# Explicit order at both ends of the SwiGLU groups of a decoder block in float32

## The chip, the cores and the metric

One core of a Trainium2 chip. The metric is the device time of one execution in microseconds (us). The engines are TensorE (PE; its weight loads are listed as PEld), VectorE (DVE), ScalarE (ACT), GpSimd (POOL) and SyncE (SP), whose queue issues nearly all loads from HBM. Each engine runs its own instructions in order; semaphores tie the engines together.

## The reference, cut to what matters

A decoder block: a mixer (pooling heads beside differential attention), then a gated feed-forward part, each with a norm before and after it. Sequence 256, width D = 2048, inner width DFF = 5632, everything in float32. The change is in the feed-forward part alone:

```python
hn = rms_norm(h, pre_ffn_norm[l])
ff = (jax.nn.silu(hn @ w_gate[l]) * (hn @ w_up[l])) @ w_down[l]
h = h + rms_norm(ff, post_ffn_norm[l])
```

## The kernel before, in words

**Split products.** A float32 product is made of three: each operand is split into a high part (a rounded copy in float32r, made by ACT) and a low part (the rest, a subtraction on DVE), and PE adds high x high, high x low and low x high. So for each tile of weights that arrives (raw), ACT writes wh, DVE writes wl, and then PE runs.

**Stages of the feed-forward part.** The 5632 inner columns are cut into 11 groups of 512. Group 0 is computed by two plain products: gate (`w_g0`) and then up (`w_u0`), by `gemm_a` (L139) with the weights split by `split` (L97) in a ring of 4 KB tiles (pool `ring`: 6 raw, 3 hi, 3 lo). Then `ring` is closed (L656) and `ring2` is opened on the same side of the memory: 3 raw, 2 wh and 2 wl of 8 KB per partition, one T of 8 KB, 2 rh and 2 rl of 6 KB, 88 KB in all.

Groups 1 to 10 run the loop at L717. A group has eight blocks j, one for each pair of k tiles; a block's weights are up and gate for two k. Blocks 0, 2 and 5 (SK) go by a scheme with seven products in place of eight: `prepare` (L700) copies the high part rh of three of the four weight tiles (ACT), builds three running sums T (three DVE additions, L708 to L710), takes rl (DVE), then sh into a wh buffer (ACT) and its low part into a wl buffer (DVE). The other five blocks take only wh and wl. `product` (L725) has the three matmuls of one term (L729 to L731) and adds into the PSUM banks m1 to m8. m1 to m4 come from the four banks "mm" that the products of group 0 use too.

At the end of a group the banks are combined on DVE (u2 to u4, sg), ACT takes the Silu, and `gated` (L659) multiplies gate by up into gg, two tiles of 128 rows. PE transposes gg in `g_parts` (L668) through the single bank m5, and ACT copies it to gT[c] (L673). For group c this is done in the middle of group c + 1. For group 0 `gated` stands after `prepare(1, 0)` (L715, L716).

**Down product.** `closing` (L527) runs four column blocks of `w_down`, each over 44 k tiles, by `gemm_a` and `mm_a` (L132). `g_split` (L792) splits gT[c] into gh and gl, four k at a time; `before_down` calls it for c = 0 to 10 at i = 0, 4, 8 and so on during the first column block, and at i = 8 it first runs `g_parts` for the last group. The tiles gh0 to gh2 lie in the pool `last`, which takes the place of the groups' temporaries (pool `ft`, closed at L774).

**What sets the order.** The instructions of each engine are put in order when the program is built, by a planner that runs a time model and takes, at each moment, what is ready in the model, earlier lines first. An order is given by hand only where `tc.issue_after(ins)` stands: what the block traces on the engine of ins is queued behind ins. A tile with `bufs=n` takes whichever of the n slots the planner finds free. A pool gives its tags addresses in the order in which they are first asked for.

Of the kernel before, what the change touches and what calls it, by code (L numbers as in the profile page):

```python
# [8 lines left out]
F32 = mybir.dt.float32  # L9
# [6 lines left out]
P = 128  # L16
# [29 lines left out]
def block_kernel(ctx: ExitStack, tc: tile.TileContext, x, xT, pos, cols, rows, lamv, invf, invcnt,  # L46
# [85 lines left out]
    def mm_a(ps, a, t, k, wh, wl, first, last):  # L132

        with tc.issue_after(behind[0]) if behind[0] is not None else nullcontext():
            mm.matmul(ps[t][:, :], lhsT=a[0](k, t), rhs=wh, start=first, stop=False)  # L135
            mm.matmul(ps[t][:, :], lhsT=a[1](k, t), rhs=wh, start=False, stop=False)  # L136
            mm.matmul(ps[t][:, :], lhsT=a[0](k, t), rhs=wl, start=False, stop=last)  # L137
# [492 lines left out]
    ft = p_ft.enter_context(tc.tile_pool(name="ft", bufs=1, reuse_waits="tile"))  # L630
    psum_m = ctx.enter_context(tc.tile_pool(name="psum_m", bufs=1, space=bass.MemoryType.PSUM, reuse_waits="tile"))
# [42 lines left out]

    def blocks(src, j):

        raw = ring2.tile([P, 4, 512], F32, tag="raw", name=nm("raw"), bufs=3)
        for half in range(2):
            s = src[j][:, half * 1024:(half + 1) * 1024].rearrange("p (a b) -> p a b", b=512)
            latest[0] = sync.dma_start(raw[:, 2 * half:2 * half + 2], s).ins  # L680
        return raw

    def low(x, hi, tag, bufs=2):
        res = ring2.tile([P, x.shape[1], 512], F32R, tag=tag, name=nm(tag), bufs=bufs)
        dve.tensor_tensor(res, x, hi.bitcast(F32), ALU.subtract)  # L685
        return res

    def high(x, tag, bufs=2):
        res = ring2.tile([P, x.shape[1], 512], F32R, tag=tag, name=nm(tag), bufs=bufs)
        act.activation(res, x, AF.Copy)  # L690
        return res
# [8 lines left out]
    def prepare(c, j):  # L700
# [5 lines left out]
        s = ring2.tile([P, 4, 512], F32, tag="T", name=nm("T"), bufs=1)  # L706
# [7 lines left out]

    ready = prepare(1, 0)  # L715
    gg = [gated(ps[t][:, :], t) for t in range(2)]  # L716
    for c in range(1, NF // 4):  # L717
# [44 lines left out]
        if c < NF // 4 - 1:  # L762
            ready = prepare(c + 1, 0)
        sg = [cp.tile([P, 512], F32, tag="gain", name=nm("sg"), bufs=2) for _ in range(2)]
# [13 lines left out]
    def of_whole(tag, dt, bufs):  # L778
        def one(half=None):
            h = whole.get((tag, "half"), 0) if half is None else half  # L780
            if h == 0:
                whole[tag] = ring2.tile([P, 4, 512], dt, tag=tag, name=nm(tag), bufs=bufs).rearrange("p a b -> p (a b)")
            whole[tag, "half"] = 1 - h
            return whole[tag][:, h * 1024:(h + 1) * 1024]
# [5 lines left out]
    gh, gl = [], []  # L790

    def g_split(c):  # L792

        gl.append(fp.tile([P, 4, 2, P], F32R, tag="g", name=f"gl{c}", bufs=NF // 4 + 1))
        for half in range(2):
            z = slice(2 * half, 2 * half + 2)
            if c < 3:
                gh.append(last.tile([P, 2, 2, P], F32R, name=f"gh{c}_{half}"))
            else:
                gh.append(half_tile("gh").rearrange("p (a b c) -> p a b c", a=2, b=2))  # L800
            with tc.issue_after(last_split[0]) if c > 0 else nullcontext():
                act.activation(gh[-1], gT[c][:, z], AF.Copy)
            dve.tensor_tensor(gl[c][:, z], gT[c][:, z], gh[-1].bitcast(F32), ALU.subtract)  # L803

    def before_down(c, i):
        if c == 0 and i % 4 == 0:
            if i == 8:
                g_parts(NF // 4 - 1, gg)
            g_split(i // 4)
# [8 lines left out]
    def mg_tile():  # L818
        n = len(mgs)
        if used[0] == n:  # L820
            three = ring2.tile([P, 3, 512], F32, tag="rh" if n % 2 == 0 else "rl", name=nm("mg"), bufs=2)
# [71 lines left out]
```

## Time and profile before

| | |
|---|---|
| median of 3 runs | 1050.13 us (1048.53 to 1050.70) |
| the profiled execution | 1049.04 us, its span 1047.2 us |
| PE busy | 1021.4 us, 98% of the span |
| PE weight loads | 843.5 us, 81% |
| DVE busy | 732.1 us, 70% |
| ACT busy | 537.5 us, 51% |
| read from HBM | 198.37 MB, written 4.19 MB |

The span runs from the first to the last instruction of one profiled execution; what the run takes beyond it lies around it. Times in the rows are microseconds from the start of the span. In the rows of the timeline a number in brackets is the idle time of that engine just before, with what ended it. A matmul of 512 columns is listed with 0.39 us although the next one starts sooner: matmuls overlap, and their starts tell the rate.

### The profile page before, as it was taken

What the parts mean: (1) busy time and instruction counts of PE and PEld (TensorE: products, weight loads), DVE (VectorE), ACT (ScalarE), POOL (GpSimd) and SP (SyncE); (2) the same over time, 40 slices, a digit from 0 to 9 for tenths busy, and PEclk for the clock granted to TensorE, in tenths of its full rate; (3) what the DMA queues carried; (4) which work ended last, traced back from release to release, by engine and by line L of the source; (5) the groups of instructions that cost most, each with busy time, mean ns of one, the idle gap of its engine ahead of it and who ended that gap; (6) DMA issues with size and microseconds to landing.
All of it is one profiled execution on the core that took longest, in us unless ns stands there. A gap on an engine that the chain in (4) does not pass through costs nothing.

```text
span 1047.2 us, 12568 instructions
## 1 busy us (share of the span) xinstructions
PE 1021.4 (98%) x4787; PEld 843.5 (81%) x4787; DVE 732.1 (70%) x847; ACT 537.5 (51%) x643; POOL 34.6 (3%) x57
## 2 busy tenths in 40 slices
PE   8999999999999899999999999999998999999996
PEld 5888888988877688888888888888886888888884
DVE  6648745875677778888798897887876664454444
ACT  6746545664547545455545555554455553343431
POOL 0003200210030000000000000000000000000000
PEclk9999999999999999999999999999998999999998
DMA  8753555456754455555555556566564575556542
GB/s 328 281 182 122 179 183 178 154 170 213 237 202 162 153 201 181 181 204 198 202 200 190 199 184 221 181 210 214 176 217 146 189 284 195 199 200 211 190 172 81
DMA packets 57517, 203.39 MB, mean 194 GB/s; under 512 B 6896, under 2 KB 7792, under 8 KB 56688
## 3 DMA queue, kind: packets, MB, share of 16 engines
q1 hardware_dynamic: 57168, 202.44, 56.1%
q8 instruction: 37, 0.61, 0.2%
q14 instruction: 24, 0.20, 0.1%
q10 hardware_dynamic: 288, 0.15, 0.1%
HBM read 198.37 MB, written 4.19 MB: 193 GB/s over the span
## 4 chain that ended last, share of the span: by engine, by line
PE 88%; DVE 6%; DMA 3%; issue 2%; ACT 1%; SPq 0%; DVEq 0%; ACTq 0%
PE mm L137 15%; PE mm L136 15%; PE mm L135 15%; PE mm L729 8%; PE mm L731 8%; PE mm L730 8%; PE tr L730 2%; PE tr L729 2%; PE tr L731 2%; DMA raw<-in_w_gu 2%; PE mm L171 2%; PE mm L173 1%; PE mm L172 1%; DVE xn L561 1%; PE m L729 1%
## 5 line engine op out<-in xcount | busy, mean ns | idle before, releaser
L100 DVE TENSOR_TENSOR wl<-raw,wh 128x1024 fp32r<-128x1024 f32 x88 | 104.7, 1222 | 112.9 <-ACT wh L99 112.9
L100 DVE TENSOR_TENSOR wlo<-raw,whi 128x1024 fp32r<-128x1024 f32 x97 | 119.2, 1229 | 70.4 <-ACT whi L99 64.0
L99 ACT ACTIVATE wh<-raw 128x1024 fp32r<-128x1024 f32 x88 | 89.3, 1052 | 128.0 <-PE mm L136 123.8
L99 ACT ACTIVATE whi<-raw 128x1024 fp32r<-128x1024 f32 x97 | 102.2, 1057 | 78.1 <-PE mm L136 60.7
L136 PE MATMUL mm<-wh,gl 128*128 128x512 f32 x352 | 138.2, 393 | 1.2 <-DVE gl L803 1.2
L135 PE MATMUL mm<-wh,gh 128*128 128x512 f32 x352 | 136.3, 392 | 0.0
L137 PE MATMUL mm<-wl,gh 128*128 128x512 f32 x352 | 131.4, 392 | 0.0
L730 PE MATMUL mm<-wh,h 128*128 128x512 f32 x330 | 128.8, 390 | 0.0
L729 PE MATMUL mm<-wh,h 128*128 128x512 f32 x330 | 128.7, 390 | 0.0
L685 DVE TENSOR_TENSOR wl<-raw,wh 128x2048 fp32r<-128x2048 f32 x50 | 114.3, 2286 | 6.8 <-ACT wh L690 6.8
L731 PE MATMUL mm<-wl,h 128*128 128x512 f32 x330 | 113.3, 393 | 0.0
L690 ACT ACTIVATE wh<-T 128x2048 fp32r<-128x2048 f32 x30 | 57.4, 1914 | 95.2 <-DVE T L694 68.9
L685 DVE TENSOR_TENSOR wl<-T,wh 128x2048 fp32r<-128x2048 f32 x30 | 68.7, 2290 | 53.5 <-ACT wh L690 53.5
L690 ACT ACTIVATE wh<-raw 128x2048 fp32r<-128x2048 f32 x50 | 95.4, 1907 | 13.4 <-issue 10.5
L136 PEld LDWEIGHTS mm<-wh,gl 128*128 128x128 f32 x352 | 66.7, 190 | 15.5 <-DVE gl L803 1.6
L135 PE MATMUL mm<-whi,x 128*128 128x512 f32 x192 | 75.1, 395 | 3.3 <-ACT whi L277 3.1
L137 PEld LDWEIGHTS mm<-wl,gh 128*128 128x128 f32 x352 | 66.8, 190 | 14.1
L135 PEld LDWEIGHTS mm<-wh,gh 128*128 128x128 f32 x352 | 66.5, 189 | 13.9
L136 PE MATMUL mm<-whi,x 128*128 128x512 f32 x192 | 75.2, 394 | 0.0
L730 PEld LDWEIGHTS mm<-wh,h 128*128 128x128 f32 x330 | 62.1, 188 | 13.0
L731 PEld LDWEIGHTS mm<-wl,h 128*128 128x128 f32 x330 | 62.0, 188 | 13.0
L729 PEld LDWEIGHTS mm<-wh,h 128*128 128x128 f32 x330 | 62.1, 188 | 12.7
(240 smaller groups left out, 1911.8 us busy)
## 6 DMA issues: line engine op xcount, KB each, us to landing
raw<-in_w_gu SPq DMA_DIRECT2D x160, 512.0 KB, 4.3
raw<-in_w_down SPq DMA_DIRECT2D x88, 512.0 KB, 4.2
raw<-in_w_in SPq DMA_DIRECT2D x46, 512.0 KB, 3.8
raw<-in_w_out SPq DMA_DIRECT2D x32, 512.0 KB, 3.7
raw<-in_w_u SPq DMA_DIRECT2D x24, 512.0 KB, 3.5
raw<-in_w_g SPq DMA_DIRECT2D x8, 512.0 KB, 5.8
xn<-in_x SPq DMA_DIRECT2D x2, 1024.0 KB, 8.9
gain<-in_rows SPq DMA_DIRECT2D x8, 256.0 KB, 4.3
```

What stands on the lines that cost most here:

```text
L99: last_split[0] = act.activation(hi, raw, AF.Copy).ins
L100: (by or dve).tensor_tensor(lo, raw, hi.bitcast(F32), ALU.subtract)
L135: mm.matmul(ps[t][:, :], lhsT=a[0](k, t), rhs=wh, start=first, stop=False)
L136: mm.matmul(ps[t][:, :], lhsT=a[1](k, t), rhs=wh, start=False, stop=False)
L137: mm.matmul(ps[t][:, :], lhsT=a[0](k, t), rhs=wl, start=False, stop=last)
L171: mm.matmul(o, lhsT=wh, rhs=xh, start=st, stop=False)
L172: mm.matmul(o, lhsT=wh, rhs=xl, start=False, stop=False)
L685: dve.tensor_tensor(res, x, hi.bitcast(F32), ALU.subtract)
L690: act.activation(res, x, AF.Copy)
L729: mm.matmul(o, lhsT=a[0], rhs=wh, start=first, stop=False)
L730: mm.matmul(o, lhsT=a[1], rhs=wh, start=False, stop=False)
L731: mm.matmul(o, lhsT=a[0], rhs=wl, start=False, stop=left[i] == 0)
```

## The change

Four edits.

1. `gated` of group 0 is queued on DVE behind the last low part of `prepare(1, 0)`.
2. `g_parts` of the last group, at i = 8 of the down product, is queued on PE behind the last matmul traced before it (`last_mm`, set in `mm_a`).
3. The split of the first four k of the down product (`g_split(0)`) moves from i = 0 of the down product to the last group, to the place where the other groups prepare the next group's first block. Its high part gets a tile of its own, gh0, in the pool `fp`. gh1 and gh2 become one tile each instead of two halves; the splits of c = 1 and later stay where they were.
4. The buffers of `ring2` become one tag for each slot (`part`): raw0, raw1, raw2, wh0, wh1 and so on, used in a fixed turn, so that the pool's addresses go by the first use of each slot: raw0, T0, rh0, rl0, wh0, wl0, then raw1, wh1, wl1, then raw2, rh1, rl1. Before, they went by tag: three raw, T, two rh, two rl, two wh, two wl.

No computation is added or removed.

```diff
--- before.py
+++ after.py
@@ -134,7 +134,9 @@
         with tc.issue_after(behind[0]) if behind[0] is not None else nullcontext():
             mm.matmul(ps[t][:, :], lhsT=a[0](k, t), rhs=wh, start=first, stop=False)
             mm.matmul(ps[t][:, :], lhsT=a[1](k, t), rhs=wh, start=False, stop=False)
-            mm.matmul(ps[t][:, :], lhsT=a[0](k, t), rhs=wl, start=False, stop=last)
+            last_mm[0] = mm.matmul(ps[t][:, :], lhsT=a[0](k, t), rhs=wl, start=False, stop=last).ins
+
+    last_mm = [None]
 
     def gemm_a(srcs, a, nk, order=None, before=lambda i: None):
         ps = [bank(), bank()]
@@ -628,6 +630,7 @@
     gT = [fp.tile([P, 4, 2, P], F32, tag="g", name=f"gT{c}", bufs=NF // 4 + 1) for c in range(NF // 4)]
     p_ft = ExitStack()
     ft = p_ft.enter_context(tc.tile_pool(name="ft", bufs=1, reuse_waits="tile"))
+    gh0 = fp.tile([P, 4, 2, P], F32R, name="gh0")
     psum_m = ctx.enter_context(tc.tile_pool(name="psum_m", bufs=1, space=bass.MemoryType.PSUM, reuse_waits="tile"))
 
     sums_h, sums_l = {}, {}
@@ -672,21 +675,30 @@
                 mm.transpose(tr[:, j * P:(j + 1) * P], gg[t][:, j * P:(j + 1) * P], ident)
             act.activation(gT[c][:, :, t, :], tr.rearrange("p (a b) -> p a b", b=P), AF.Copy)
 
+    turn = {}
+
+    def part(tag, n, dt, bufs=2):
+
+        turn[tag] = (turn.get(tag, -1) + 1) % bufs
+        return ring2.tile([P, n, 512], dt, tag=f"{tag}{turn[tag]}", name=nm(tag), bufs=1)
+
     def blocks(src, j):
 
-        raw = ring2.tile([P, 4, 512], F32, tag="raw", name=nm("raw"), bufs=3)
+        raw = part("raw", 4, F32, 3)
         for half in range(2):
             s = src[j][:, half * 1024:(half + 1) * 1024].rearrange("p (a b) -> p a b", b=512)
             latest[0] = sync.dma_start(raw[:, 2 * half:2 * half + 2], s).ins
         return raw
 
-    def low(x, hi, tag, bufs=2):
-        res = ring2.tile([P, x.shape[1], 512], F32R, tag=tag, name=nm(tag), bufs=bufs)
-        dve.tensor_tensor(res, x, hi.bitcast(F32), ALU.subtract)
+    def low(x, hi, tag):
+        res = part(tag, x.shape[1], F32R)
+        last_low[0] = dve.tensor_tensor(res, x, hi.bitcast(F32), ALU.subtract).ins
         return res
 
-    def high(x, tag, bufs=2):
-        res = ring2.tile([P, x.shape[1], 512], F32R, tag=tag, name=nm(tag), bufs=bufs)
+    last_low = [None]
+
+    def high(x, tag):
+        res = part(tag, x.shape[1], F32R)
         act.activation(res, x, AF.Copy)
         return res
 
@@ -703,7 +715,7 @@
         if j not in SK:
             wh = high(raw, "wh")
             return wh, low(raw, wh, "wl")
-        s = ring2.tile([P, 4, 512], F32, tag="T", name=nm("T"), bufs=1)
+        s = part("T", 4, F32, 1)
         rh = high(raw[:, 1:4], "rh")
         tt(s[:, 0:2], raw[:, 1:3], raw[:, 0:1].to_broadcast([P, 2, 512]), ALU.add)
         tt(s[:, 2], s[:, 0], raw[:, 2], ALU.add)
@@ -712,8 +724,22 @@
         sh = high(s, "wh")
         return rh, rl, sh, low(s, sh, "wl")
 
+    gh, gl = [], []
+
+    def g_split(c, hi, after=None):
+
+        lo = fp.tile([P, 4, 2, P], F32R, tag="g", name=f"gl{c}", bufs=NF // 4 + 1)
+        for half in range(2):
+            z = slice(2 * half, 2 * half + 2)
+            gh.append(hi[half] if isinstance(hi, list) else hi[:, z])
+            with tc.issue_after(after) if after else nullcontext():
+                act.activation(gh[-1], gT[c][:, z], AF.Copy)
+            dve.tensor_tensor(lo[:, z], gT[c][:, z], gh[-1].bitcast(F32), ALU.subtract)
+        gl.append(lo)
+
     ready = prepare(1, 0)
-    gg = [gated(ps[t][:, :], t) for t in range(2)]
+    with tc.issue_after(last_low[0]):
+        gg = [gated(ps[t][:, :], t) for t in range(2)]
     for c in range(1, NF // 4):
         m = {1: bank(), 2: bank(), 3: bank(), 4: bank(), 5: None, 6: bank2(), 7: psum_m.tile([P, 512], F32, tag="m7", name=nm("m7"), bufs=1), 8: bank2()}
         n_s, n_n = len(SK), NKD // 2 - len(SK)
@@ -761,6 +787,8 @@
                 g_parts(c - 1, gg)
         if c < NF // 4 - 1:
             ready = prepare(c + 1, 0)
+        else:
+            g_split(0, gh0)
         sg = [cp.tile([P, 512], F32, tag="gain", name=nm("sg"), bufs=2) for _ in range(2)]
         for t, (i, u) in enumerate(((2, s1), (4, u3))):
             tt(sg[t], m[i][:, :], u, ALU.add)
@@ -779,7 +807,7 @@
         def one(half=None):
             h = whole.get((tag, "half"), 0) if half is None else half
             if h == 0:
-                whole[tag] = ring2.tile([P, 4, 512], dt, tag=tag, name=nm(tag), bufs=bufs).rearrange("p a b -> p (a b)")
+                whole[tag] = part(tag, 4, dt, bufs).rearrange("p a b -> p (a b)")
             whole[tag, "half"] = 1 - h
             return whole[tag][:, h * 1024:(h + 1) * 1024]
         return one
@@ -787,26 +815,15 @@
     raw_of[0] = of_whole("raw", F32, 3)
     two = of_whole("wh", F32R, 2), of_whole("wl", F32R, 2)
     parts_of[0] = lambda: (two[0](), two[1]())
-    gh, gl = [], []
-
-    def g_split(c):
-
-        gl.append(fp.tile([P, 4, 2, P], F32R, tag="g", name=f"gl{c}", bufs=NF // 4 + 1))
-        for half in range(2):
-            z = slice(2 * half, 2 * half + 2)
-            if c < 3:
-                gh.append(last.tile([P, 2, 2, P], F32R, name=f"gh{c}_{half}"))
-            else:
-                gh.append(half_tile("gh").rearrange("p (a b c) -> p a b c", a=2, b=2))
-            with tc.issue_after(last_split[0]) if c > 0 else nullcontext():
-                act.activation(gh[-1], gT[c][:, z], AF.Copy)
-            dve.tensor_tensor(gl[c][:, z], gT[c][:, z], gh[-1].bitcast(F32), ALU.subtract)
-
     def before_down(c, i):
-        if c == 0 and i % 4 == 0:
-            if i == 8:
+        if c == 0 and i == 8:
+            with tc.issue_after(last_mm[0]):
                 g_parts(NF // 4 - 1, gg)
-            g_split(i // 4)
+        if c == 0 and i % 4 == 0 and i > 0:
+            n = i // 4
+            hi = last.tile([P, 4, 2, P], F32R, name=f"gh{n}") if n < 3 else [
+                half_tile("gh").rearrange("p (a b c) -> p a b c", a=2, b=2) for _ in range(2)]
+            g_split(n, hi, last_split[0])
         if c == 1 and i == 0:
             for t in range(2):
                 xn[t] = last.tile([P, D], F32, name=f"x{t}")
@@ -818,7 +835,7 @@
     def mg_tile():
         n = len(mgs)
         if used[0] == n:
-            three = ring2.tile([P, 3, 512], F32, tag="rh" if n % 2 == 0 else "rl", name=nm("mg"), bufs=2)
+            three = part("rh" if n % 2 == 0 else "rl", 3, F32)
             mgs.extend(three[:, i] for i in range(3))
         used[0] += 1
         return mgs[used[0] - 1]
```

## Rows read from the trace of the kernel before

**Rows 1.** The page, busy time of each engine, share of the span, instructions.

```profile
PE 1021.4 (98%) x4787; PEld 843.5 (81%) x4787; DVE 732.1 (70%) x847; ACT 537.5 (51%) x643; POOL 34.6 (3%) x57
```

**Rows 2.** Timeline of PE early in the down product: start, duration, instruction.

```profile
800.53 0.39 PE L136 MATMUL mm<-wh,gl 128*128 128x512 f32 x1
...
807.58 0.39 PE L137 MATMUL mm<-wl,gh 128*128 128x512 f32 x1
```

**Rows 3.** Busy time by stretch: length, each engine's busy time, clock, DMA share, GB/s.

```profile
356.00:366.00 10.00, 5.34 (x19) 3.75 (x18) 7.64 (x7) 4.06 (x3) 0.00 (x0) 0.87 0.28 90
...
786.00:796.00 10.00, 6.84 (x32) 5.17 (x31) 9.33 (x13) 7.03 (x11) 0.00 (x0) 0.87 0.53 180
...
820.00:880.00 60.00, 60.00 (x267) 49.67 (x266) 34.58 (x36) 31.16 (x42) 0.00 (x0) 1.00 0.68 241
```

**Rows 4.** Waits of PE over the span: total us, times, longest us.

```profile
PE mm L731 <- DVE rl L685: 3.0, 1, 3.0
...
PE mm L729 <- ACT rh L690: 0.2, 1, 0.2
```

**Rows 5.** Timeline of PE at the start of group 1.

```profile
356.77 0.39 PE L729 MATMUL mm<-rh,h 128*128 128x512 f32 x1
...
363.91 0.79 PE L729 MATMUL m<-wh,sh 128*128 128x512 f32 x1 [1.64 <-ACT wh L690]
...
366.92 0.39 PE L730 MATMUL m<-wh,sl 128*128 128x512 f32 x1
```

**Rows 6.** Timeline of PE from the last group to the down product.

```profile
787.78 0.60 PE L672 MATMUL m<-ident,gg 128*128 128x128 f32 x4
788.14 0.48 PE L730 MATMUL mm<-wh,h 128*128 128x512 f32 x1
...
789.61 0.60 PE L672 MATMUL m<-ident,gg 128*128 128x128 f32 x4
792.17 0.66 PE L672 MATMUL m<-ident,gg 128*128 128x128 f32 x4 [1.96 <-DVE wl L100]
...
794.62 0.80 PE L136 MATMUL mm<-wh,gl 128*128 128x512 f32 x1 [1.21 <-DVE gl L803]
```

**Rows 7.** Timeline of DVE at the start of group 1.

```profile
351.78 0.69 DVE L650 TENSOR_TENSOR sl<-hs,sh 128x512 fp32r<-128x512 f32 x1
356.29 1.43 DVE L661 SCALAR_TENSOR_TENSOR gg<-mm,rstd,sg 128x512 f32<-128x512 f32 x2 [3.83 <-PE mm L137]
357.64 1.22 DVE L694 TENSOR_TENSOR T<-raw 128x1024 f32<-128x1024 f32 x1
...
363.89 2.29 DVE L685 TENSOR_TENSOR wl<-T,wh 128x2048 fp32r<-128x2048 f32 x1 [2.04 <-ACT wh L690]
```

**Rows 8.** Timeline of ACT at the start of group 1.

```profile
351.02 1.48 ACT L690 ACTIVATE rh<-raw 128x1536 fp32r<-128x1536 f32 x1
361.94 1.91 ACT L690 ACTIVATE wh<-T 128x2048 fp32r<-128x2048 f32 x1 [9.44 <-DVE T L694]
```

**Rows 9.** Timeline of SP's DMA queue before group 1.

```profile
336.57 3.67 SPq L680 DMA_DIRECT2D raw<-in_w_gu  x6
```

**Rows 10.** The page, DMA issues: queue, count, KB each, median us to landing.

```profile
raw<-in_w_gu SPq DMA_DIRECT2D x160, 512.0 KB, 4.3
```

**Rows 11.** Timeline of ACT from the last group to the down product.

```profile
783.67 2.01 ACT L99 ACTIVATE wh<-raw 128x1024 fp32r<-128x1024 f32 x2 [4.20 <-PE tr L730]
...
789.63 2.00 ACT L99 ACTIVATE wh<-raw 128x1024 fp32r<-128x1024 f32 x2
...
792.02 2.18 ACT L802 ACTIVATE gh<-gT 128x512 fp32r<-128x512 f32 x4
```

**Rows 12.** Timeline of DVE from the last group to the down product.

```profile
784.76 2.36 DVE L100 TENSOR_TENSOR wl<-raw,wh 128x1024 fp32r<-128x1024 f32 x2 [1.59 <-ACT wh L99]
...
792.75 1.22 DVE L100 TENSOR_TENSOR wl<-raw,wh 128x1024 fp32r<-128x1024 f32 x1
793.88 2.49 DVE L803 TENSOR_TENSOR gl<-gT,gh 128x512 fp32r<-128x512 f32 x4
```

## The prediction, made before the changed kernel was run

> **What bounds the kernel now.** I read the page first: TensorE (PE) is busy for 98% of the span, 1021.4 of 1047.2 us, so an edit can win only where PE stands still or runs slowly, about 26 us in all [rows 1]. The Trainium skill (Perfetto Trace Analysis, Identifying the Most-Contended Engine) says that matmul busy time is a bad measure of headroom and that weight-load busy time should be read instead; its 81% here would leave some 200 us. The rows speak against so much: from 820 to 880, where PE never stands, weight loads are busy for 49.67 of 60 us, 83% [rows 3], so a full stream shows hardly more than the 81%. What a full stream is, the starts tell: 32 matmuls begin from 800.53 to 807.58, 0.227 us apart [rows 2].
>
> Next, the table by stage. The two poor stretches of the feed-forward part are 356 to 366 (5.34 busy of 10, clock 0.87) and 786 to 796 (6.84 of 10, clock 0.87) [rows 3]. Those are the two ends that the change touches. Third, PE's waits: 3.0 us for rl and 1.6 for wh at the first [rows 4, 5], 2.0 before a transpose and 1.2 for gl at the second [rows 6]. In the ten groups between, the list has only 0.2 for an rh [rows 4]. Behind all four stands the queue of VectorE (DVE), once by way of ScalarE (ACT). The rest of PE's idle time lies at the start and the tail of the kernel, untouched.
>
> **The price of each end, from starts of matmuls.** Busy time hides slow matmuls, so I count starts. First end: 16 matmuls start from 356.77 until the one at 366.92 [rows 5]; at 0.227 they need 3.63 us, they took 10.15: **6.5 us** lost. Some 1.4 of it is not waiting but slow running after it: from 363.91 seven matmuls start before the one at 366.92, 3.01 us where 1.59 would do, most of them at the lower of the two clock levels, 1.2 against 2.4 GHz. Last end: from 789.61 to 800.53 two sets of four transposes (0.36 a set, from 787.78 to 788.14) and 16 matmuls start, which need 0.72 + 3.63 = 4.35; they took 10.92: **6.6 us** lost [rows 2, 6]. Both together, 13.1 us, are the most these ends can give back. The Trainium skill (TensorE: Matmul & The Clock Gate, Back-to-back issue gap) gives about 131 ns as the sustained spacing at 512 columns; by it 32 matmuls would need 4.2 us instead of 7.3 and the ends would hold 16.2. The row has 0.227, and the sum goes by the row.
>
> **First end, part by part.** DVE is free at 352.47 (0.69 after 351.78) and idles 3.83 us, because the two gg products at the head of its queue wait for the last matmul of the up projection; T, ready to run, stands behind them [rows 7]. That raw had landed is shown by ACT, which reads it for rh at 351.02 [rows 8]. The edit puts gg behind the first wl. No instruction is added; the chain T, T, rl, T, wh, wl starts at 352.47 instead of 357.64. By its own rows it takes 8.54 us (357.64 to 363.89 + 2.29), so wl ends at 361.0, wh at 358.7 (361.94 + 1.91, 5.17 earlier), rl, which stands ahead of the last T, before wh begins at 356.8, and gg (1.43 for two) follows at 361.0 to 362.4.
>
> What is late next? The first block has 21 matmuls from 356.77, 4.76 us, to 361.5 if nothing waits. Products 1 and 2 need rh and rl: there in time, until 358.1. Products 5, 6 and 7 need wh: 0.55 us late. Their low parts come up at 360.0, and wl ends at 361.0: 0.97 late. Products 3 and 4 accumulate in the PSUM banks that the up projection holds until gg has read them; they come up at 361.7 and 362.4, when gg's two halves end at 361.75 and 362.4. The block ends at 363.1, 1.6 us over. So the added wait costs 1.6 and the first end gives 6.5 - 1.6 = **4.9**. Upper bound 6.5: the three T ahead of rl (1.66 earlier), or matmuls of the next block in the holes. Lower bound 3.0: PE at the lower clock in spite of the short holes (1.4 again), and 0.5 for the third load, below.
>
> **Ring placement.** The old ring held 12 tiles of 4 KB per partition, the new one is 88 KB on the same side, so 40 KB of it lie beside the old ring. Before, three raw, T and one rh lay there, and the first rl, wh and wl on old slots; the first three blocks' six loads were issued in one run at 336.57 [rows 9]. Now raw0, T, rh, rl and wh of the first block lie there, and wl half on an old raw slot: nothing in the chain above waits for the old ring's last matmuls. The price is on SP, in order: raw1 lies on old raw slots and goes out when their splits have ended, by 352.5 at the latest, when DVE is free; raw2 lies on old weight slots and goes out after the last matmul of the up projection, 357, with raw3 behind it [rows 7, 9]. Landing takes 4.3 us in the median: 356.8 and 361.3 [rows 10]. Block 1 is wanted at 363.1, and DVE comes to block 2's T after gg and block 1's wl, at 364.7, so 3.5 us cover raw2. Landing late, it would cost what exceeds that, bounded at 0.5 by the hole that a wl may leave at block 2. The fixed turn of slots (raw 3, the others 2) replaces the choice of whichever is free; the instructions stay. I take 0 for it, between -1 and the rival below.
>
> **Last end, part by part.** PE stands at 792.17 for the transposes of the last gg, and at 794.62 for gl, whose first half is last in DVE's queue behind wl, gg, wl, 793.88 + 0.62 = 794.5 [rows 6, 12]. (a) The split of the first four k moves into the last group: two ACT copies (2.18 / 4 = 0.55 each) into an idle 4.20 us before 783.67, and two DVE subtractions (0.62 each) into an idle 1.59 before 784.76 [rows 11, 12]. Hidden there; without that cover they would delay a wl by 1.2. The new gh0 tile needs no space of the group's temporaries, which is why it can be early. (b) The last transposes go behind the 48 matmuls of k = 0 to 7: 0.72 us on PE at either place, and their result is wanted only at k = 40. (c) So after 789.97 PE finds wh (785.7), wl (787.1), gh and gl of k = 0 to 3 ready and runs 24 matmuls to 795.4. Late next: the second source, whose wh end at 791.6 and wl at 793.97 [rows 11, 12], and gl1, 0.62 and 1.24 later, 794.6 and 795.2. They are wanted at 795.4 and 796.8, so 0.8 us are over. The gain is 6.6 less 0.1 = **6.5**; the lower bound is 4.0, if gl1 falls behind by its own 1.24 and the clock drops once more (1.4). The SP load of gain that waits for gg, and the w_down loads behind it, keep their place: the fifth source is wanted at k = 16, 812, and issued at 794.
>
> **Sum.** 4.9 + 6.5 = 11.4 us. The profiled execution took 1049.04 (span 1047.2 and 1.84 around), 1.09 under the median of 1050.13. It would come to 1037.6, and the median to **1038.7**.
>
> **Rivals.**
> - Banks: PE's queue has product 3 ahead of the low products. Then PE stands from 357.5 until the first gg ends at 361.75, 4.3 us, with 1.4 of low clock; the first end gives 0.8 and the time is 1042.8. For: before, product 3's matmuls stood second, right behind gg. Against: whoever orders PE knows that gg now comes after wl.
> - Last end half: gl1 and the second source late, 1.24 and 1.4 of clock, say 2.6: 1041.3. For: DVE is busy for 9.33 of 10 us there [rows 3]. Against: 1.24 us of that is moved away.
> - Slower: the fixed turn binds a split to the buffer used two tiles ago in program order. If the work runs in another order, each of the 10 groups waits for one more wl, 2.29 us [rows 7]: 22.9 lost, 1061.6. It decides from 1.14 us a group. For: PE already waits 0.2 us for a late rh inside the groups [rows 4], so the loop from wl to raw to rh has no slack. Against: a turn among equal buffers is what a full ring does anyway.
> - It does nothing: T at 352.47 waits for something that no row shows, and the transposes were not what held PE: 1050. Against: rh at 351.02.
>
> **How the numbers follow.** Forecast 0.60, with its own range 1036.5 to 1041; banks 0.17; half of the last end 0.10; slower 0.08; nothing 0.05. The range 1035.5 to 1043.5 takes in the first three (0.87, less a little at the edges) and leaves out the last two. A measurement of this kernel tells 0.2% (2.1 us) from no change: faster 0.87, same 0.05, slower 0.08.
>
> **What would show it.** Right: DVE starts T near 352.5 and gg near 361; PE's waits for rl and wh shrink from 4.6 us to under 2; the matmuls after the last group start at once, the waits for gl and before the transposes are gone, and no 0.43 gaps stand near 795. Wrong: a wait of PE on gg at the head, a wait on gl at k = 4, SP's loads of block 2 landing after 364.7, or waits on rh or wh that grow in every group.

## The result and the profile after

The changed kernel takes 1041.2 us in the median of 4 runs (1040.3 to 1042.6); the kernel before, in 4 runs, 1049.7. The ratio is 0.992, with a 95% interval of 0.9903 to 0.9938. 11.4 us of gain were forecast, and 8.5 came.

The profiled execution took 1042.59 us, span 1040.8, against 1049.04 and 1047.2: 6.4 us less. It is the longest of the four; the other three had spans from 1038.5 to 1039.7. I cut TensorE's stream in three: the **head** from the first matmul of group 1 to the start of ACT's first copy of s1 (behind block 5 of group 1), the **groups** from there to the last matmul of group 10, and the **end** from there to the last matmul of the down product.

| us | head | groups | end | sum |
|---|---|---|---|---|
| before | 29.66 | 402.95 | 247.17 | 679.78 |
| after | 24.23 | 408.85 | 240.83 | 673.91 |
| difference | -5.43 | +5.90 | -6.34 | -5.87 |

Group 1 also starts 0.59 earlier (356.18 against 356.77), which makes the 6.4. So both ends gave what was forecast (4.9 and 6.5), and the ten groups between, for which the forecast had 0, took 5.9 back.

Busy time by stretch of the changed kernel, with columns as in [rows 3]:

```profile
356.00:366.00 10.00, 9.53 (x41) 7.31 (x40) 9.27 (x8) 3.41 (x2) 0.00 (x0) 1.00 0.87 298
786.00:796.00 10.00, 10.00 (x50) 8.26 (x49) 9.50 (x13) 6.06 (x9) 0.00 (x0) 1.00 0.54 171
```

PE now stands for 0.5 us in the one stretch and not at all in the other, and the clock is 1.00 in both, where [rows 3] has 0.87. What has gone wrong is in PE's waits from 356 to 800, all there are (us in total, times, longest):

```profile
PE mm L757 <- DVE wl L695: 3.8, 4, 1.2
PE mm L755 <- ACT rh L702: 0.5, 1, 0.5
```

The four waits for wl are new. The timeline shows what stands around one of them, in group 4, in the order of time.

```profile
504.06 1.22 DVE L706 TENSOR_TENSOR T<-raw 128x1024 f32<-128x1024 f32 x1
505.32 0.69 DVE L706 TENSOR_TENSOR T<-T,raw 128x512 f32<-128x512 f32 x1
505.93 2.29 DVE L695 TENSOR_TENSOR wl<-raw,wh 128x2048 fp32r<-128x2048 f32 x1
...
508.24 1.75 SPq L690 DMA_DIRECT2D raw<-in_w_gu  x4
...
518.21 1.49 ACT L702 ACTIVATE rh<-raw 128x1536 fp32r<-128x1536 f32 x1 [3.82 <-DMA raw<-in_w_gu]
519.60 1.90 ACT L702 ACTIVATE wh<-raw 128x2048 fp32r<-128x2048 f32 x1
...
523.46 2.28 DVE L695 TENSOR_TENSOR wl<-raw,wh 128x2048 fp32r<-128x2048 f32 x1
...
525.79 0.50 PE L757 MATMUL mm<-wl,h 128*128 128x512 f32 x1 [1.17 <-DVE wl L695]
```

Read it from the end. PE waits 1.17 us for the low half of block 7 (wl, 523.46), which DVE takes from the high half that ACT made at 519.60. ACT had it behind the copy for the next group's block 0, and that copy waited 3.82 us for its load. The two loads, of block 7 and of the next block 0, left SP's queue in one run at 508.24. The first of them takes the raw buffer of block 4, and DVE took the low half of block 4 at 505.93, behind two of the three sums T of block 5; before the change it stood behind one. Before, the load of block 7 left some 2 us before the copy of s1, now 1.0 us after it.

So the planner ordered the groups otherwise than before. The order on the two engines in each of groups 2 to 10, by blocks:

```
before  ACT wh.2 wh.3       DVE wl.2 wl.3  T.5 rl.5 wl.4 T.5 T.5
after   ACT wh.3 wh.2       DVE wl.3 wl.2  rl.5 T.5 T.5 wl.4 T.5
```

The rows of group 4 show it. In the kernel before, ACT's copy from T (block 2) comes ahead of the one from raw (block 3), and the low half of block 4 (510.35) has two sums behind it:

```profile
501.18 1.92 ACT L690 ACTIVATE wh<-T 128x2048 fp32r<-128x2048 f32 x1 [2.93 <-PE tr L730]
503.00 1.90 ACT L690 ACTIVATE wh<-raw 128x2048 fp32r<-128x2048 f32 x1
...
507.55 1.22 DVE L694 TENSOR_TENSOR T<-raw 128x1024 f32<-128x1024 f32 x1
508.68 1.75 DVE L685 TENSOR_TENSOR rl<-raw,rh 128x1536 fp32r<-128x1536 f32 x1
510.35 2.28 DVE L685 TENSOR_TENSOR wl<-raw,wh 128x2048 fp32r<-128x2048 f32 x1
512.55 1.41 DVE L694 TENSOR_TENSOR T<-T,raw 128x512 f32<-128x512 f32 x2
```

In the changed kernel the copy from raw comes first; the DVE rows stand above:

```profile
495.58 1.92 ACT L702 ACTIVATE wh<-raw 128x2048 fp32r<-128x2048 f32 x1 [2.84 <-PE tr L756]
497.40 1.90 ACT L702 ACTIVATE wh<-T 128x2048 fp32r<-128x2048 f32 x1
```

Two things differ: block 3 is made ahead of block 2 (the **exchange**), and the low half of block 4 stands behind two sums (the **late low half**). No line of the change names either.

### The profile page after: what moved, and what is told of

It is laid out like the page before. It is cut to its first block, busy times and chain, and to the rows that moved or that the text cites. A ratio compares the mean times of both kernels' runs of the same rounds, so it can differ in the third digit from the quotient of the medians.

```text
span 1040.8 us, 12565 instructions
## 1 busy us (share of the span) xinstructions
PE 1018.6 (98%) x4787; PEld 839.4 (81%) x4787; DVE 733.4 (70%) x847; ACT 538.8 (52%) x643; POOL 34.6 (3%) x57
## 4 chain that ended last, share of the span: by engine, by line
PE 85%; DMA 6%; DVE 6%; issue 1%; SPq 1%; ACT 1%; DVEq 0%; ACTq 0%
PE mm L137 15%; PE mm L136 15%; PE mm L135 15%; PE mm L757 8%; PE mm L755 7%; PE mm L756 7%; DMA raw<-in_w_gu 4%; PE tr L757 2%; PE tr L756 2%; PE tr L755 2%; DVE wl L695 2%; PE mm L173 2%; PE mm L175 2%; PE mm L174 1%; PE m L755 1%; DVE xn L563 1%
## 5 line engine op out<-in xcount | busy, mean ns | idle before, releaser
L757 PE MATMUL mm<-wl,h 128*128 128x512 f32 x330 | 115.6, 394 | 3.8 <-DVE wl L695 3.8
```

The source lines that it names most:

```text
L757: mm.matmul(o, lhsT=a[0], rhs=wl, start=False, stop=left[i] == 0)
```

## Experiments

Head, groups and end are cut as in the table above; times are medians, ratios are against the kernel before, with 95% intervals. Line numbers differ by a few from kernel to kernel. Where an expectation gives the groups some 425 to 440 us, it counts from the first matmul of group 1 to the last of group 10, head and groups of the table together.

| run | head | groups | end | time | ratio |
|---|---|---|---|---|---|
| e1_no_turn | 26.58 | 413.01 | 240.82 | 1050.6 | 1.0010 (0.9997 to 1.0023) |
| e2_turn_only | 27.72 | 407.89 | 246.15 | 1051.0 | 1.0016 (1.0000 to 1.0032) |
| e3_in_order | 26.55 | 419.91 | 240.82 | 1058.0 | 1.0085 (1.0058 to 1.0111) |
| e4_end_only | 29.85 | 402.13 | 240.82 | 1043.3 | 0.9943 (0.9927 to 0.9960) |
| e5_pin_turn | 24.20 | 414.76 | 240.82 | 1047.4 | 0.9994 (0.9983 to 1.0006) |
| e6_pin_free | 26.58 | 402.10 | 240.83 | 1038.6 | 0.9902 (0.9887 to 0.9916) |
| e7_flip | 24.21 | 404.25 | 240.82 | 1037.9 | 0.9900 (0.9883 to 0.9917) |
| e8_tail | 24.08 | 416.17 | 240.83 | 1050.5 | 1.0014 (1.0005 to 1.0024) |
| e9_stay | 22.60 | 404.57 | 240.82 | 1036.7 | 0.9884 (0.9868 to 0.9899) |
| e10_seven | 24.17 | 415.71 | 242.59 | 1051.0 | 1.0029 (1.0018 to 1.0039) |
| e11_two_lines | 24.39 | 403.57 | 240.82 | 1039.0 | 0.9903 (0.9887 to 0.9920) |
| e12_stay_late | 24.07 | 402.03 | 240.82 | 1036.3 | 0.9886 (0.9867 to 0.9904) |

The copy of s1, where head and groups meet, starts between the 102nd and the 103rd matmul of group 1 in most of these kernels. In e1, e3 and e6, where ACT has another order in group 1, it starts six or seven matmuls later, and in e9 eight earlier. If all are cut at the 102nd matmul, the others change by 0.2, and these four have heads of 25.0, 24.9, 24.9 and 24.2 and groups of 414.6, 421.6, 403.8 and 403.0.

### First four: parts of the change

**The change without the fixed turn of the ring buffers.** In `part`:

```
-        turn[tag] = (turn.get(tag, -1) + 1) % bufs
-        return ring2.tile([P, n, 512], dt, tag=f"{tag}{turn[tag]}", name=nm(tag), bufs=1)
+        return ring2.tile([P, n, 512], dt, tag=tag, name=nm(tag), bufs=bufs)
```

> The first three edits without the fourth: the buffers of ring2 keep one tag for each kind, placed by kind and taken as they come free. Theory A: both ends gave what they hold, and the fixed turn of wh and wl lets block 3 of a group go ahead of block 2 on ACT and DVE, which costs the groups some 6.5 us. Then this takes 1035 us (8.5 us gained by the whole change, plus 6.5), PE has no wait on a wl in the groups, and a group takes 42.7 us as before. Theory B: the groups lose because PE comes to them 6 us earlier and DVE and the loads have less lead, whatever the buffers. Then 1041, with the same waits on wl. Theory C: the placement by first use is what the first end lives on. Then the first block waits for wl as before and the time is 1040 or more, with a stall of 3 us or more near 357.

**The fixed turn alone**, all else as in the kernel before.

> The fourth edit alone: fixed turn and placement by first use, neither end ordered. Theory A: the groups lose the 6.5 us and nothing is won: 1056, and as wl of block 1 stands ahead of wl of block 0 at the first end, up to 2.3 more. Theory B: the groups keep 42.7 us and the time is that of before, 1050. Theory C: the placement alone gives part of the first end: 1045 to 1050.

**The whole change, block 3 forced behind block 2 on ACT**: each wh is queued behind the wh traced before it.

```
+        with tc.issue_after(last_wh[0]) if tag == "wh" and last_wh[0] else nullcontext():
+            ins = act.activation(res, x, AF.Copy).ins
...
```

> The whole change, and in addition each wh of the groups is queued on ACT behind the wh traced before it; buffers, turn and placement stay. Theory A: the order of blocks 2 and 3 alone costs the groups their 6.5 us, so 1035 us, with no wait of PE on wl in the groups. If it is the placement or the turn itself, as buffers, or the missing lead of theory B, the time stays at 1041.

**The edits of the last end alone** (the early split, the transposes behind last_mm), buffers as before.

> The last end alone (second and third edit): the transposes of the last gg behind the first matmuls of the down product, and the split of its first four k in the last group. By the sum of the prediction it gives 6.5 us, 1043.2, and the groups stay at 42.7 us each under every theory. If the two ends only pay together, less than 4.

The last end is settled: alone it takes 6.35 us from the end (247.17 to 240.82) and leaves the groups as they were, 402.13 against 402.95. The fixed turn alone brings most of the groups' loss by itself, 407.89, with the same exchange and the same late low half in the planned order, and PE waits 3.3 us in 4 waits for wl. Its head gains 1.9 and its end 1.0, which is why its time is not the 1056 that the first theory asked for.

But the other two fit no forecast. By my first theory, that the turn costs by way of the exchange, the groups were to come back to some 403; without the turn they took 413, and with block 3 held back by force 420. PE's waits in these two, first the kernel without the turn:

```profile
PE mm L756 <- DVE wl L694: 4.7, 6, 1.3
PE m L754 <- ACT gT L676: 2.2, 5, 0.5
```

and the kernel with block 3 held back:

```profile
PE m L760 <- ACT gT L676: 5.0, 9, 0.7
PE mm L760 <- ACT wh L703: 4.3, 4, 1.4
PE mm L762 <- DVE wl L695: 3.7, 6, 0.8
```

In both the planner had found a third order for the groups: ACT takes the high half of block 5 ahead of the copy of s1, and in most groups block 2's rh ahead of gT or sg. Their groups last 38 to 41 and 47 to 51 us, mostly in turn, where the kernel before has 42.5 to 43.0. So these two say nothing yet about the turn. The kernel without the turn differs from the one with the last end alone (groups 402.13, in the order of before) by the first edit alone: an edit at the head, made once, reorders 400 us behind it. From here on I wrote the order of the groups out by hand, so that only one thing changed at a time.

### Second four: the order written out

A list of ACT's and one of DVE's work per group, for groups 2 to 10, each instruction queued behind the one before it in the list:

```
+    def pin(order):
+        was = None
+        for c in range(2, NF // 4):
+            for label in order.format(q=c - 2, p=c - 1, c=c, n=c + 1).split():
...
+                    tc.add_manual_dep(ins, was.name, mybir.DependencyInfo(
+                        mybir.DependencyClass.NoSync, mybir.DependencyReason.DATA), reason="order")
...
+    pin("wh{c}.1 rh{c}.2 gT{q} gT{q} wh{c}.2 wh{c}.3 rh{c}.5 wh{c}.4 s1{c} wh{c}.5 wh{c}.6 rh{n}.0 wh{c}.7 wh{n}.0 asg{c} asg{c}")
...
```

**The order of before, buffers in the fixed turn.**

> The whole change as it is, buffers in a fixed turn included; only the order of ScalarE's and VectorE's work inside groups 2 to 10 is written out by hand, as it stood in the kernel before (block 2 ahead of block 3, the low half of block 4 ahead of the last two sums of block 5). Theory O (the lost microseconds lie in the order that the planner chose for the groups, and in nothing else): from the first to the last matmul of the groups 426.3 us instead of 433.1, group period 42.5 to 42.9 as before the change, no wait of 1.2 us on the low half of block 7, time 1034 to 1037 us. Theory L (groups lose because TensorE comes to them some 6 us earlier and DMA and VectorE have less lead): the groups stay at 432 to 434 us, time 1040 to 1042. Theory F (buffers in a fixed turn cost by themselves): the groups stay at 432 to 434 us, and the next kernel, with free buffers, gains.

**The order of before, buffers free.** The same lists, `part` as in the kernel without the turn.

> As the last kernel, but with the ring buffers as before (any free buffer of a name). Theory O: as the last kernel, 1034 to 1037 us; group 1, which is not written out, may lose up to 2 us, since the planner orders it otherwise here. Theory L: 1040 to 1042, as the last. Theory F: 1034 to 1037, with the last kernel at 1040 or more.

**The fixed turn with the exchange alone.** In the lists, `wh{c}.3 wh{c}.2` and `wl{c}.3 wl{c}.2`.

> As the first kernel of these four, but block 3 is made ahead of block 2 on ScalarE and VectorE, as the planner had it in the changed kernel; the low half of block 4 stays ahead of the last two sums of block 5. Theory O with the whole cost in this exchange (the buffer that the low half of block 4 needs is that of block 2, which TensorE then reads last): groups 432 to 433 us, time 1040 to 1041.5. Theory O with the whole cost in the place of the low half of block 4: groups 426 to 427, time 1034 to 1037. Theories L and F: no difference from the first kernel, both at 1040 to 1042.

**The fixed turn with the late low half alone.** In DVE's list, `rl{c}.5 T{c}.5 T{c}.5 wl{c}.4 T{c}.5`.

> As the first kernel of these four (block 2 ahead of block 3), but the low half of block 4 stands behind two of the three sums of block 5, as the planner had it in the changed kernel. Theory O with the cost in the exchange of blocks 2 and 3: 1034 to 1037 us. Theory O with the cost here: VectorE makes the low half of block 4 some 1.2 us later, the load of block 7 starts as much later, groups 429 to 433 us, time 1037 to 1041. Theories L and F: as the first kernel, 1040 to 1042.

With free buffers the order of before gives 402.10 in the groups, with the fixed turn 414.76. PE's waits of the latter (window 355 to 800):

```profile
PE m L763 <- ACT wh L709: 10.3, 9, 1.1
PE mm L765 <- DVE wl L700: 0.6, 1, 0.6
PE mm L763 <- ACT rh L709: 0.5, 1, 0.5
```

Nine waits of 1.1 us for a wh, one in each of the nine groups whose order is written out. One of them, PE first and then ACT:

```profile
498.25 0.39 PE L763 MATMUL m<-wh,sh 128*128 128x512 f32 x1
498.48 0.39 PE L764 MATMUL m<-wh,sl 128*128 128x512 f32 x1
...
500.92 0.50 PE L763 MATMUL m<-wh,sh 128*128 128x512 f32 x1 [1.15 <-ACT wh L709]
...
498.95 1.91 ACT L709 ACTIVATE wh<-T 128x2048 fp32r<-128x2048 f32 x1 [4.50 <-PE m L764]
```

ACT could have made block 2's wh (498.95) 4.5 us earlier, but waits for the matmul at 498.48. That is product 5 of block 0: it adds into bank m5, which the transposes of gg hold first (the planner has put those of group c's gg into the first blocks of group c + 2). So PE takes it last of its block, among the first matmuls of block 2 and just ahead of those that read block 2's wh. Under the turn block 2 has the buffer of block 0, which is read until then. Before the change a tile took whichever buffer was free: in the compiled program block 2's wh lies at the same address as block 1's (172000 for both in group 4), in the changed kernel at that of block 0 (135136). So the exchange is the planner's way around this wait, and a good one: with it alone the groups take 404.25, 10.5 less, and none of the nine waits is left. The late low half alone has all nine (10.3 us) and 416.17; beside the exchange, in the changed kernel, it costs 408.85 - 404.25 = 4.6.

No theory had the first and the last of the four: they took 1047.4 and 1050.5, and the slowest forecast was 1042. I had the exchange down as a loss, and under the turn it is a gain. Of the other two theories, that PE comes too early for the loads falls with the free buffers (402.10), and that the turn costs by itself was nearest, but as one buffer, not as a price of the places.

### Last four: the one buffer, and the queues

**The turn stands still at block 2**, nothing else is changed and no order is written out.

```
+        stay = tag in ("wh", "wl") and at[0] == SK[1]
+        turn[tag] = (turn.get(tag, -1) + (not stay)) % bufs
...
```

> The whole change, fixed turn included, with no order written out; only the turn of the high and low halves stands still at block 2, so that block 2 takes the two buffers of block 1, as the planner had placed it in the kernel before, and not those of block 0, of which TensorE reads the last matmuls just ahead of block 2. Theory B2 (the buffer of block 2 is the root: it makes the planner put block 3 ahead, and the late low half of block 4 follows from that): the planner goes back to the order of before in groups 2 to 10, no wait on the low half of block 7, groups 428 to 429 us, time 1037 to 1039. Rival (the fixed turn costs in another way too, by the other buffers or their places): groups 431 us or more, time 1040 or more.

**Block 7 ahead of the next block 0**, the changed kernel's own order otherwise: `wh{c}.7 rh{n}.0` on ACT and `wl{c}.6 wl{c}.7 T{n}.0` on DVE.

> The changed kernel with its own order in groups 2 to 10 written out, block 3 ahead of 2 and the late low half of block 4 included; only block 7 stands ahead of the next group's block 0 on ScalarE and VectorE. Theory Q (the 1.2 us waits on the low half of block 7 come from the queues: ScalarE waits some 3.8 us for the next group's load with block 7's copy behind it): these waits go, groups 428.5 to 430 us, time 1037 to 1039. Rival (the load of block 7 itself lands too late, since its buffer waits for the low half of block 4): the waits stay or move, groups 432 to 434, time 1040 to 1042.

**Two sums behind the low half**, the exchange left as it is:

```
+        with tc.issue_after(last_low[0]) if j == SK[-1] else nullcontext():
             tt(s[:, 2], s[:, 0], raw[:, 2], ALU.add)
             tt(s[:, 3], s[:, 2], raw[:, 3], ALU.add)
```

> The changed kernel with one thing asked of the planner: the last two sums of block 5 stand behind the low half of block 4 on VectorE. Block 3 stays ahead of block 2. Theory T (under the fixed turn the late low half of block 4 is what costs): as the run with the exchange alone, groups 428.5 to 430 us, time 1037.5 to 1039. Rival (the order had to be that of the first run in every step, the first sum of block 5 ahead of its low half included): waits of some 0.3 to 0.6 us a group, groups 431 to 434, time 1040 to 1042.

**The turn stands still at block 2 from group 2 on**: as the first of these four, with `at[0] = j if c > 1 else None`.

> As the run in which the turn stands still at block 2, but only from group 2 on; group 1 keeps the turn and the order of the changed kernel. The planned order of all engines in the groups is then that of the run with the order of before written out and a plain turn, instruction by instruction; only the buffers of block 2 differ between the two. Theory B2: the 1.1 us wait of every group on the high half of block 2 is gone, group period 42.5 to 42.6, groups 1 to 3 as fast as in the run with the late sums (108.2 us from the first group matmul to the third copy of s1, where the turn standing still from group 1 took 110.6), groups 424.5 to 426.5 us, time 1033.5 to 1036. Rival (the order alone sets the time): as the run with the written order and a plain turn, groups 438 to 440 us, time 1046 to 1049.

With block 2 on the buffers of block 1 the planner goes back to the order of before in groups 2 to 10 of its own accord, and the time is 1036.7. The last run is the sharpest: on PE, ACT and DVE its order is that of the first kernel with the order written out, instruction by instruction, and only the choice between equal buffers differs: block 2 takes the wh and wl of block 1, and so block 3 those of block 0, where the plain turn gives block 2 those of block 0 and block 3 those of block 1. Its groups take 402.03 against 414.76, and this is all of PE's waits from 350 to 800:

```profile
PE mm L757 <- ACT rh L703: 0.4, 1, 0.4
```

ACT's copy of block 2 there, in the same group, is let go by block 1's last reading of its wh, and ends at 497.3, before PE wants it at 497.66:

```profile
495.42 1.92 ACT L703 ACTIVATE wh<-T 128x2048 fp32r<-128x2048 f32 x1 [2.91 <-PE tr L758]
```

With 1036.3 us, 0.9886 of before (0.9867 to 0.9904), this kernel beats both; it is the change and some five lines more.

The two sums held back also work: no wait for wl is left, groups 403.57. As whole-kernel times the three cures (1036.3, 1036.7, 1039.0) and the exchange alone (1037.9) lie within 3 us.

The run with block 7 ahead is a miss, 1051.0 where 1042 was the slowest forecast. The waits for wl are gone, as expected, but others came:

```profile
PE m L763 <- ACT gT L676: 5.5, 8, 0.7
PE mm L763 <- ACT wh L709: 1.5, 8, 0.2
```

PE now waits for gT in each of groups 3 to 10, as product 5 waits for bank m5, and the end is 1.8 us longer. Moving block 7 ahead was paid with later work on both engines, so this run doesn't tell the queue's share from the load's.

**How the late low half costs, and what stays open.** In the changed kernel the load of block 7 and that of the next block 0 leave 0.91 us apart in groups 2 to 9, since the low half of block 4 and the last sum of block 5, which free their buffers, follow each other; with the low half ahead of two sums it is 1.33. From issue to the start of ACT's copy, for which ACT always waits there, the next block 0 takes, in groups 3 to 9:

| | apart | issue to copy |
|---|---|---|
| the changed kernel | 0.91 | 7.30 to 9.05, mostly late in every second group |
| the turn alone | 0.91 | 7.38 to 9.09 |
| the late low half alone | 0.91 | 7.38 to 9.01 |
| before, the last end alone, the order of before (turn, free), the exchange alone, two sums held back, the turn standing still (both) | 1.33 | 6.77 to 7.61 |

So it is not the late issue alone: with two sums held back the load of block 7 leaves at nearly the same point (0.8 us after the copy of s1, against 1.0) and no group waits for wl. In groups 4, 6, 8 and 9 of the changed kernel, the four with the wait, the time from one copy of s1 to the next is 43.5 to 44.2 us; in groups 3, 5 and 7 it is 42.8, as it is in the exchange alone in each of groups 3 to 9. So the 4.6 us lie in those four groups.

The distance of the two loads doesn't decide it by itself. In group 2, which the table leaves out, loads 1.33 us apart take 7.46 to 8.90 as well; and in the kernel without the turn and the one with block 3 held back, loads of groups 3 to 9 that are 0.91 apart take only 7.26 to 7.60. What a late load looks like is seen in 40 slices of 0.25 us from 508 to 518, in GB/s, first of the changed kernel:

```profile
GB/s 0 0 0 0 115 66 229 344 311 131 180 164 180 344 360 426 442 344 410 426 410 360 328 295 393 328 426 344 311 279 180 197 49 0 16 0 33 16 66 49
```

and of the exchange alone, whose copy starts at 516.46:

```profile
GB/s 0 0 0 0 98 131 295 344 213 147 147 279 311 344 492 377 426 410 393 492 377 393 361 328 344 393 360 361 229 164 147 98 0 0 0 0 0 0 0 82
```

In the first a few packets still come from 516 to 517.5, after the stream has ended; the copy starts at 518.21. (What comes last in both rows may belong to the next load.) The DMA view of the changed kernel shows what was moved besides, first from 515.3 to 516.25, then from 516.25 to 517.69 (queue: packets, MB, share of the 16 DMA engines):

```profile
q8 instruction: 1, 0.02, 6.1%
...
q1 hardware_dynamic: 7, 0.02, 4.6%
```

By the times of the single packets in the trace, one packet of 16 KB, of the queue that the profile calls instruction, runs from 515.31 to 516.24. The last six 4 KB packets of the load then run one behind another, from 516.23 to 517.68, as if one DMA engine had to move the 16 KB first (the trace doesn't name a packet's engine). In the exchange alone such a packet starts at 515.89, when all but the last packets of the load are through, and the load lands at 516.37.

In all 14 kernels one such packet falls between the issue of block 7's load and the landing of the next block 0 in each of groups 2, 4, 6 and 8, and in no odd group. Of the 112 loads of a next block 0 (groups 2 to 9), 15 landed 8.2 us or more after their issue. 14 of these are in even groups, and in 13 at least five packets of the load run right behind the 16 KB. So nearly all of the late loads go with this meeting, and when it happens differs with the order of the work; no run here moved the packet by itself. Open are group 9 of the changed kernel (8.23, no such packet), group 4 of the late low half alone (the packet is there, but nothing of the load runs right behind it), and why loads 0.91 apart meet it so much more often in groups 4 to 8. (In the run with block 7 ahead ACT comes to that copy late for its own reasons, so it is not in the table.)

## Why the prediction was right, and where it was wrong

**Bound and prices of the ends: right.** 16 matmuls of the head's start took 10.15 us and now take 3.82, at 0.227 each 3.63 [rows 5]. At the last end the gap before the first down matmul fell from 3.31 to 0.23.

**First end: the way was right, the size within 0.5.** T starts at 351.81 and gg at 360.34 (forecast 352.5 and 361; 0.6 of the difference is group 1 starting earlier):

```profile
351.81 1.22 DVE L706 TENSOR_TENSOR T<-raw 128x1024 f32<-128x1024 f32 x1
...
355.94 2.29 DVE L695 TENSOR_TENSOR wl<-raw,wh 128x2048 fp32r<-128x2048 f32 x1
358.14 2.28 DVE L695 TENSOR_TENSOR wl<-T,wh 128x2048 fp32r<-128x2048 f32 x1
360.34 1.40 DVE L664 SCALAR_TENSOR_TENSOR gg<-mm,rstd,sg 128x512 f32<-128x512 f32 x2
```

The gain is 5.4, not 4.9. The 1.6 us of waits on wh, wl and the banks mostly didn't come, since the planner took block 1's split (355.94) ahead of block 0's and let PE fill the hole with block 1's matmuls, which the forecast had only as its upper bound. That order is worth 0.6 to 1.1 us and comes from the fixed turn: up to the 102nd matmul, the three runs with the head's edit in which block 0 stays first (free buffers, or forced) take 24.9 to 25.0, those with block 1 first 23.9 to 24.2, and the kernel before 29.5. With block 0 first, as the forecast had it, the end gives 4.5, and PE is 2.0 us behind its pitch by then, where the forecast had 1.6. The third load, bounded at 0.5, costs that:

```profile
362.46 0.50 PE L755 MATMUL mm<-rh,h 128*128 128x512 f32 x1 [0.47 <-ACT rh L702]
```

ACT has block 2's raw at 360.92; 361.3 was forecast.

**Last end: right.** 6.5 forecast, 6.34 measured. The first matmul of the down product follows in PE's pitch, and gl of k = 0 to 3 is taken inside the last group; no 0.43 gap is left near 795:

```profile
789.27 0.39 PE L757 MATMUL tr<-wl,h 128*128 128x512 f32 x1
789.50 0.62 PE L135 MATMUL mm<-wh,gh 128*128 128x512 f32 x2
...
788.13 1.28 DVE L737 TENSOR_TENSOR gl<-gT,gh 128x512 fp32r<-128x512 f32 x2
```

**Ring placement: the step that failed** is "I take 0 for it, between -1 and the rival below", on the fixed turn of slots. Its ground was the sentence under the slower rival, that a turn among equal buffers is what a full ring does anyway. The runs show that it isn't: block 2 had taken the buffer of block 1, not the one used two tiles ago, because block 0's is read last. The rival itself had the right mechanism (a split bound to the buffer used two tiles ago, if work runs in another order), but took it for PE's wait at a price of 2.29 us a group. The price would have been a wait of 1.1 a group on PE, and 12.7 us over the groups as written out by hand (414.76 - 402.03), had the planner not dodged it; by dodging it paid 408.85 - 402.03 = 6.8 in the profiled execution, most of it (4.6) for the late low half, which the forecast had no term for. The forecast used a list of PE's waits, which has nothing of who holds which buffer, and [rows 4] can't show a wait that the free choice avoids.

Of the other rivals, the banks held by gg cost nothing: product 3 got a free bank and ran at 356.64, and products 2 and 4, which the planner gave the held ones, stood behind other work of PE. The last end gave all of its share. That the time lay within the range is in part luck: its upper side was there for these two, neither of which came, and the loss came from the rival that the range leaves out. It fitted in since it stayed under the 1.14 us a group from which that rival decides: 0.6.

Put right, the sum holds: with block 2 on block 1's buffers, as before, 5.6 (head) + 0.9 (groups) + 6.35 (end) = 12.9 us of the trace, and 12.5 between the medians of the runs side by side (1048.8 and 1036.3), where 11.4 was forecast.

The Trainium skill (Perfetto Trace Analysis, Optimization Strategy) says of the same gap coming again and again on the engine that should be saturated that it can mean too little memory for the next tile, in buffer count or tile size. The nine equal waits of 1.1 us agree that a tile waits for its buffer; but the last run has the same number of buffers and none of the waits, so here it was which buffer, not how many.

## What to carry to other kernels

A rotation written by hand is not the same as a ring that takes any free buffer: before fixing a turn, look in the compiled program at which buffer each tile took, and at which engine reads the old one last. Where a planner orders the work, an edit at one end can reorder everything behind it, so compare the planned order of the untouched loop before costing it at nothing. And write that order out by hand when two effects have to be told apart: the choice between two equal buffers then moved the groups by 12.7 us with the same instructions in the same order.

## What was not expected of the hardware

A single 16 KB packet of the queue called instruction, 0.93 us long, that falls into the last part of a load went with a late end of that load: in group 4 of the changed kernel six 4 KB packets of the load ran one by one behind it, and ACT got the load 9.05 us after its issue, where 6.8 to 7.6 were usual. Such a packet came in groups 2, 4, 6 and 8 of every kernel here, and in 13 of the 15 latest loads packets ran right behind it.
